# Down and row products issued as two matmuls of 256 columns in place of one of 512

## The chip, the cores and the metric

The kernel runs on one core of one Trainium2 chip. The metric is the device time of one execution in microseconds. Three runs of the kernel before gave 1739.73 to 1748.12 us, median 1745.62. Times in the profile are microseconds unless marked ns.

## The reference

One sequence of 256 tokens with 1024 features in float32 passes through two layers and then a second block. Cut to what matters here (the mixers between are recurrences, convolutions and attention over projections of the same kind):

```python
def swiglu(h, w_gate, w_up, w_down):
    return (jax.nn.silu(h @ w_gate) * (h @ w_up)) @ w_down        # 1024 -> 2816 -> 1024

for layer in range(2):                                            # first block
    x = x + 0.5 * swiglu(rmsnorm(x, norm_ffn1[layer]), ffn1_gate[layer], ffn1_up[layer], ffn1_down[layer])
    x = x + hybrid_mixer(rmsnorm(x, norm_mix[layer]), ...)
    x = x + 0.5 * swiglu(rmsnorm(x, norm_ffn2[layer]), ffn2_gate[layer], ffn2_up[layer], ffn2_down[layer])
h = rmsnorm(x, norm_final)                                        # second block, one layer
...                                                               # retention and dilated attention -> mixed
h = h + rmsnorm_2(mixed @ w_o[i], g_post_mix[i])
v2 = rmsnorm_2(h, g_pre_mlp[i])
f = jnp.square(jax.nn.relu(v2 @ w_up[i])) @ w_down[i]             # 1024 -> 4096 -> 1024
h = h + rmsnorm_2(f, g_post_mlp[i])
gate = jax.nn.sigmoid(rmsnorm_2(h, g_pre_ple[i]) @ w_ple_gate[i] + b_ple_gate[i])
e = p[i].astype(h.dtype) @ w_ple_in[i]
h = h + rmsnorm_2(gate * e, g_post_ple[i])
```

## The kernel before

**Products in three parts.** Every float32 operand of a large product is split into a rounded part and the rest (`xh`, `xl` for tokens, `wh`, `wl` for weights, type float32r), and a product is three matmuls: `xh wh + xh wl + xl wh`. `wchunk` (lines 86 to 95) brings weights in chunks of two k-tiles (2 x 128 rows, up to 512 columns, 512 KB): a DMA on SyncE's queue into one of four `raw` tiles, a cast on ScalarE to `wh` (line 93) and a subtraction on VectorE to `wl` (line 94), three pairs deep.

**Two ways to multiply.** `gemm_feat` (line 170) gives features on partitions: the stationary operand is a block of 128 weight columns, the moving one all 256 tokens, so each matmul has 256 columns; two outputs share a PSUM bank of 512 columns (lines 186 to 188). It is used for gate and up products of the FFNs, the MLP's up product and many projections. `gemm_tok` (line 121) gives tokens on partitions: the stationary operand is 128 tokens, the moving one up to 512 weight columns, so each matmul has 512 columns and fills a bank (lines 141 to 143 in `mm_tok`). Each matmul is issued with a weight load of its own, also where its stationary operand is the one before.

**Where the change touches.** Down products: `ffn` (line 314) runs four times; behind its feature products it computes two column halves of 512, each over 22 k-tiles and both token halves, with `gemm_tok` (line 348), and adds them to the residual. When the first column half is added, the next norm's transposes (line 279) of it can run, in the middle of the second half. Row products: `gemm_rows` (line 145) computes all 1024 columns into four banks, token half after token half in the last three chunks (`tail`), whose weights are kept in the room of hidden tiles (`hT`), so that the first token half is finished early. It is called for the output projection (`combine`, 8 k-tiles), the MLP's down product (`mlp`, 32 k-tiles) and the gate of the last part (`ple`, 8 k-tiles). All other users of `gemm_tok` (mixer and second block's projections, lines 571, 583, 1195, 1215, 1310 to 1358, 1420) keep their form.

**Order.** The program is written for a framework that tracks dependences, places instructions on the engines with a simulated timeline and the order of the program as priority, and adds the semaphores. TensorE runs its matmuls in the order placed.

Of the kernel before, what the change touches and what calls it, by code (L numbers as in the profile page):

```python
# [18 lines left out]
KC = 2  # L19
# [32 lines left out]
class Ctx:  # L52
# [65 lines left out]
        return self.m4.tile([P, 1040], F32, tag="m4", name=self.nm(name))  # L118


    def gemm_tok(self, xs, w, kt0, nkt, c0, n, outs=None, first=True, last=True, wk0=0):

        nc = self.nc
        xs = xs if isinstance(xs, list) else [xs]
        if outs is None:
            outs = [self.mm_tile() for _ in range(2)]
        for g in range(0, nkt, KC):
            m = min(KC, nkt - g)
            wh, wl = self.wchunk(w, (wk0 + g) * P, m, c0, n)
            for t in range(2):  # L130
                self.mm_tok(outs[t][:, :n], xs, kt0 + g, m, t, wh, wl, first and g == 0, last and g + m == nkt)
        return outs

    def mm_tok(self, o, xs, kt0, m, t, wh, wl, a, z):

        nc = self.nc
        tok = slice(t * P, (t + 1) * P)
        for k in range(m):
            xh, xl = xs[(kt0 + k) // 8]
            kt = (kt0 + k) % 8  # L140
            nc.tensor.matmul(o, xh[:, kt, tok], wh[:, k], start=a and k == 0, stop=False)  # L141
            nc.tensor.matmul(o, xh[:, kt, tok], wl[:, k], start=False, stop=False)  # L142
            nc.tensor.matmul(o, xl[:, kt, tok], wh[:, k], start=False, stop=z and k == m - 1)  # L143

    def gemm_rows(self, xs, w, nkt, tail, js):

        xs = xs if isinstance(xs, list) else [xs]
        outs = [[self.mm_tile() for _ in range(2)] for _ in range(2)]  # L150
        ng = nkt // KC
        for g in range(ng - tail):
            for ch in range(2):
                wh, wl = self.wchunk(w, g * KC * P, KC, ch * 512, 512)
                for t in range(2):
                    self.mm_tok(outs[ch][t], xs, g * KC, KC, t, wh, wl, g == 0, False)
        room = []
        for j in js:
            pair = [a.rearrange("p a b -> p (a b)").rearrange("p (i k c) -> p i k c", i=2, k=KC) for a in self.hT_tile(j)]
            room += [(pair[0][:, i], pair[1][:, i]) for i in range(2)]  # L160
        room += [None] * (2 * tail - len(room))
        ws = [[self.wchunk(w, g * KC * P, KC, ch * 512, 512, room.pop(0)) for g in range(ng - tail, ng)] for ch in range(2)]
        for t in range(2):
            for ch in range(2):
                for i, g in enumerate(range(ng - tail, ng)):
                    self.mm_tok(outs[ch][t], xs, g * KC, KC, t, *ws[ch][i], g == 0, g == ng - 1)
        return outs


# [136 lines left out]
def hidden_split(c, hT, hc, f0, nb):  # L306

    k0 = f0 // P
    h, l = hT[k0 // 8]
    k0 %= 8  # L310
    c.split(h[:, k0:k0 + nb], l[:, k0:k0 + nb], hc)


def ffn(c, st, wT, wg, wu, wd, F):


    nc = c.nc
    xs, r = st.norm_T(wT)
    between = []
    rbc = r_broadcast(c, r, between)  # L320
    rq = c.small.tile([P, 2], F32, tag="rr", name=c.nm("rr"))
    nc.vector.tensor_scalar(rq, r, 0.25, None, op0=ALU.mult)
    KF = F // P
    hT = [c.hT_tile(j) for j in range((KF + 7) // 8)]
    rb = bc(rbc.unsqueeze(1), [P, 2, S])
    for c0 in range(0, F, 512):
        n = min(512, F - c0)
        g = c.gemm_feat(xs, wg, 8, c0, n)
        gs = []

        def gate():
            for i in range(n // 256):
                gn, th = v2(c.w2("gn"), 2), v2(c.w2("th"), 2)
                nc.vector.tensor_tensor(gn, v2(g[i], 2), rb, op=ALU.mult)
                nc.scalar.activation(th, gn, AF.Tanh, scale=0.5)
                nc.vector.scalar_tensor_tensor(th, th, 1.0, gn, op0=ALU.add, op1=ALU.mult)
                gs.append(th)

        if c0 == 0:
            between.append(gate)  # L340
        else:
            gate()
        u = c.gemm_feat(xs, wu, 8, c0, n, between)
        for i in range(n // 256):
            nc.vector.tensor_tensor(gs[i], gs[i], v2(u[i], 2), op=ALU.mult)
            hidden_split(c, hT, gs[i], c0 + 256 * i, 2)
    for c0 in (0, 512):
        o = c.gemm_tok(hT, wd, 0, KF, c0, 512)
        for t in range(2):
            xx = st.x[:, t, c0:c0 + 512]  # L350
            nc.vector.scalar_tensor_tensor(xx, o[t], rq[:, t:t + 1], xx, op0=ALU.mult, op1=ALU.add)
# [38 lines left out]
def bc(ap, shape):  # L390
    return ap.broadcast_to(list(shape))
# [95 lines left out]
def r_broadcast(c, r, later=None):  # L487

    nc = c.nc
    ps = c.x_tile("rbc")  # L490
    h, l = (c.small.tile([P, 2, P], F32R, tag=n, name=c.nm(n), bufs=1) for n in ("dgh", "dgl"))
    for t in range(2):
        nc.scalar.activation(h[:, t], c.ident, AF.Copy, scale=r[:, t:t + 1])
        nc.vector.scalar_tensor_tensor(l[:, t], c.ident, r[:, t:t + 1], h[:, t].bitcast(F32), op0=ALU.mult, op1=ALU.subtract)
    o = c.small.tile([P, S], F32, tag="rbcs", name=c.nm("rbcs"))
    f = lambda a: a.rearrange("p a b -> p (a b)")
    nc.tensor.matmul(ps[:, :S], c.onesr, f(h), start=True, stop=False)

    def rest():
        nc.tensor.matmul(ps[:, :S], c.onesr, f(l), start=False, stop=True)  # L500
        nc.scalar.copy(o, ps[:, :S])

    rest() if later is None else later.append(rest)
    return o


def v2(ap, a):
    return ap.rearrange("p (a b) -> p a b", a=a)
# [985 lines left out]
def block_kernel(tc, a, layout):  # L1494
    with ExitStack() as stack:
        c = Ctx(tc, stack)
        nc = c.nc
        st = Stream(c, a["x"])
        cols = load_cols(c, a["col"], layout)
        for L in range(2):  # L1500
            wn = lambda n: cols[n][:, 8 * L:8 * L + 8]
            ffn(c, st, wn("norm_ffn1"), a["ffn1_gate"][L], a["ffn1_up"][L], a["ffn1_down"][L], D_FF)
            if L == 0:
                load_consts(c, a["tab"])
                prm = MixParams(c, cols, a, a)
                fq = c.const.tile([P, 9], F32, name="fq")
                o = TAB2_LAYOUT["invf"][0]
                nc.gpsimd.dma_start(fq, a["tab2"][:, o:o + 9])
                rope = Rope(c, a["pos_row"], a["pos_col"], fq[:, 0:1], fq[:, 1:9])
            Mixer(c, st, prm, a["w_in"][L], a["w_out"][L], L)  # L1510
            ffn(c, st, wn("norm_ffn2"), a["ffn2_gate"][L], a["ffn2_up"][L], a["ffn2_down"][L], D_FF)
        Block2(c, st, prm, a, rope)
# [41 lines left out]
```

## Time and profile before

| | |
|---|---|
| median of three runs | 1745.62 us |
| the profiled execution | 1734.22 us |
| its span, first to last instruction | 1732.4 us |
| TensorE matmuls / weight loads busy | 98% / 88% |
| VectorE, ScalarE busy | 68%, 53% |
| read from memory | 289 MB, 168 GB/s over the span |

A row of the page's groups has the line, engine and operation, what is written and read, the shape, the count, and then busy time and mean duration in ns. A matmul's recorded duration is longer than its distance to the next one, since matmuls are pipelined; the distance between starts gives the rate. PEld is the weight load, which can lie beside the matmul before it. Some matmul records can be missing.

### The profile page before, as it was taken

Reading aid. Unit: us, or ns where it says so; the run is one execution under the profiler, and the core shown is the slowest. Engines: PE = TensorE matmul, PEld = TensorE weight load, DVE = VectorE, ACT = ScalarE, POOL = GpSimd, SP = SyncE. Lnnn points to the kernel's source line nnn. Section 1 sums busy time; section 2 is a strip of 40 time slices with the busy share of each in tenths; the row PEclk is TensorE's granted clock in tenths of the full one; section 3 lists DMA queues with packets and bytes.
Section 4 is the critical chain, followed back from the end, with each engine's and each line's share of the span. In section 5 each row is a group of like instructions: output and inputs, shape, how many; then the busy total and the mean of one; then the engine's idle time right before and its main releaser. Section 6 shows DMA issues by size and latency. Waiting matters only on the chain.

```text
span 1732.4 us, 28619 instructions
## 1 busy us (share of the span) xinstructions
PE 1696.1 (98%) x11266; PEld 1529.2 (88%) x11266; DVE 1175.7 (68%) x2099; ACT 909.8 (53%) x1420; POOL 24.8 (1%) x62
## 2 busy tenths in 40 slices
PE   8999999999999999999989999999999999999996
PEld 7998899889988998899879998888888888799885
DVE  7666689776655765589866656656666665766467
ACT  5445576554444544568545445555454544555454
POOL 2000000100000000000000000000000000000000
PEclk9999999999999999999999999999999999999998
DMA  7657543345475656543435565554434456556661
GB/s 232 196 162 229 173 146 90 105 137 194 157 230 184 195 177 209 171 153 108 144 108 191 184 201 190 176 181 147 144 122 129 154 180 215 192 170 193 188 228 61
DMA packets 90503, 292.12 MB, mean 169 GB/s; under 512 B 9568, under 2 KB 22240, under 8 KB 90368
## 3 DMA queue, kind: packets, MB, share of 16 engines
q1 hardware_dynamic: 89648, 289.12, 51.6%
q8 instruction: 88, 1.44, 0.3%
q0 software_dynamic: 576, 1.07, 0.3%
q14 instruction: 47, 0.39, 0.1%
q10 hardware_dynamic: 144, 0.11, 0.0%
HBM read 289.21 MB, written 1.05 MB: 168 GB/s over the span
## 4 chain that ended last, share of the span: by engine, by line
PE 88%; DVE 5%; ACT 4%; issue 1%; DMA 1%; DVEq 0%; ACTq 0%
PE mm L141 14%; PE mm L142 13%; PE mm L143 13%; PE mm L187 13%; PE mm L188 13%; PE mm L186 13%; PE sv L730 1%; ACT wh L93 1%; DVE wl L94 1%; DMA raw<-in_weights 1%; PE pv L1268 1%; PE dsc L1236 1%; PE dsc L1235 1%; PE dpT L1254 0%; PE dS L677 0%
## 5 line engine op out<-in xcount | busy, mean ns | idle before, releaser
L94 DVE TENSOR_TENSOR wl<-raw,wh 128x1024 fp32r<-128x1024 f32 (+2 forms) x544 | 640.0, 1177 | 447.1 <-ACT wh L93 444.9
L93 ACT CAST wh<-raw 128x1024 fp32r<-128x1024 f32 (+2 forms) x544 | 550.4, 1013 | 608.1 <-PE mm L187 258.6
L186 PE MATMUL mm<-xTh,wh 128*128 128x256 f32 x2112 | 584.9, 279 | 4.0 <-ACT xTh L200 2.9
L187 PE MATMUL mm<-xTl,wh 128*128 128x256 f32 x2112 | 587.1, 279 | 1.3 <-DVE xTl L201 1.2
L188 PE MATMUL mm<-xTh,wl 128*128 128x256 f32 x2112 | 585.6, 279 | 0.1
L186 PEld LDWEIGHTS mm<-xTh,wh 128*128 128x128 f32 x2112 | 397.1, 189 | 8.4 <-ACT xTh L200 4.6
L187 PEld LDWEIGHTS mm<-xTl,wh 128*128 128x128 f32 x2112 | 398.2, 189 | 4.2 <-DVE xTl L201 3.1
L188 PEld LDWEIGHTS mm<-xTh,wl 128*128 128x128 f32 x2112 | 397.2, 189 | 2.1 <-issue 1.2
L142 PE MATMUL mm<-wl,hT 128*128 128x512 f32 x608 | 240.0, 395 | 0.0
L143 PE MATMUL mm<-wh,hT 128*128 128x512 f32 x608 | 237.1, 392 | 0.0
L141 PE MATMUL mm<-wh,hT 128*128 128x512 f32 x608 | 218.4, 395 | 2.8 <-ACT hT L200 2.7
L142 PE MATMUL mm<-wl,xTh 128*128 128x512 f32 (+1 forms) x440 | 168.9, 385 | 0.0
L143 PE MATMUL mm<-wh,xTl 128*128 128x512 f32 (+1 forms) x440 | 165.7, 382 | 0.1
L141 PE MATMUL mm<-wh,xTh 128*128 128x512 f32 (+1 forms) x440 | 160.0, 383 | 1.5 <-ACT xTh L200 1.5
L141 PEld LDWEIGHTS mm<-wh,hT 128*128 128x128 f32 x608 | 114.5, 189 | 28.3 <-ACT hT L200 3.5
L143 PEld LDWEIGHTS mm<-wh,hT 128*128 128x128 f32 x608 | 114.7, 189 | 25.5 <-DVE hT L201 0.9
L142 PEld LDWEIGHTS mm<-wl,hT 128*128 128x128 f32 x608 | 114.7, 189 | 24.0
L141 PEld LDWEIGHTS mm<-wh,xTh 128*128 128x128 f32 x440 | 82.0, 188 | 18.3 <-ACT xTh L200 2.4
L142 PEld LDWEIGHTS mm<-wl,xTh 128*128 128x128 f32 x440 | 82.8, 188 | 16.4 <-issue 1.9
L143 PEld LDWEIGHTS mm<-wh,xTl 128*128 128x128 f32 x440 | 82.4, 188 | 16.5 <-issue 2.0
L200 ACT ACTIVATE xTh<-xtr,colp 128x256 fp32r<-128x256 f32 (+1 forms) x72 | 28.9, 450 | 14.0 <-DVE xTl L201 12.4
L201 DVE SCALAR_TENSOR_TENSOR xTl<-xtr,colp,xTh 128x256 fp32r<-128x256 f32 (+1 forms) x72 | 30.5, 448 | 3.7 <-ACT xTh L200 3.4
(456 smaller groups left out, 1590.0 us busy)
## 6 DMA issues: line engine op xcount, KB each, us to landing
raw<-in_weights SPq DMA_DIRECT2D x514, 512.0 KB, 3.4
raw<-in_weights SPq DMA_DIRECT2D x32, 256.0 KB, 3.2
raw<-in_weights SPq DMA_DIRECT2D x16, 260.0 KB, 3.2
x_res<-in_x SPq DMA_DIRECT2D x4, 256.0 KB, 5.9
rowp<-in_b_gate SPq DMA_DIRECT2D x2, 512.0 KB, 4.0
out<-pg SPq DMA_DIRECT2D x4, 256.0 KB, 2.1
tab<-in_tab SPq DMA_DIRECT2D x1, 900.5 KB, 5.4
ctab<-in_tab POOLq DMA_DIRECT2D x1, 643.0 KB, 6.4
```

The lines of the kernel that those rows point to most:

```text
L93: nc.scalar.copy(h, raw)
L94: nc.vector.tensor_tensor(l, raw, h.bitcast(F32), op=ALU.subtract)
L141: nc.tensor.matmul(o, xh[:, kt, tok], wh[:, k], start=a and k == 0, stop=False)
L142: nc.tensor.matmul(o, xh[:, kt, tok], wl[:, k], start=False, stop=False)
L143: nc.tensor.matmul(o, xl[:, kt, tok], wh[:, k], start=False, stop=z and k == m - 1)
L186: nc.tensor.matmul(o, wh[:, k, cs], xh[:, kt], start=a, stop=False)
L187: nc.tensor.matmul(o, wh[:, k, cs], xl[:, kt], start=False, stop=False)
L188: nc.tensor.matmul(o, wl[:, k, cs], xh[:, kt], start=False, stop=z)
L200: nc.scalar.activation(h, src, AF.Copy, scale=scale)
L201: nc.vector.scalar_tensor_tensor(l, src, scale, h.bitcast(F32), op0=ALU.mult, op1=ALU.subtract)
L730: nc.tensor.matmul(o[:, h], lhsT[:, h], rhs[:, h], start=True, stop=True)
L1235: nc.tensor.matmul(ps[:, 0:P], q[:, 0:P], k[:, 0:P], start=True, stop=True)
```

## The change

`mm_tok` gets a number of pieces, `cut`; with `cut=2` each matmul of 512 columns becomes two of 256 columns, with the same stationary operand, into the two halves of the same bank. The start mark stands on the first piece of a bank's first product alone, the stop mark on the last piece of its last. `gemm_tok` passes `cut` on (default 1); the down products and both loops of `gemm_rows` ask for 2.

```diff
-    def gemm_tok(self, xs, w, kt0, nkt, c0, n, outs=None, first=True, last=True, wk0=0):
+    def gemm_tok(self, xs, w, kt0, nkt, c0, n, outs=None, first=True, last=True, wk0=0, cut=1):
...
-                self.mm_tok(outs[t][:, :n], xs, kt0 + g, m, t, wh, wl, first and g == 0, last and g + m == nkt)
+                self.mm_tok(outs[t][:, :n], xs, kt0 + g, m, t, wh, wl, first and g == 0, last and g + m == nkt, cut)
...
-    def mm_tok(self, o, xs, kt0, m, t, wh, wl, a, z):
+    def mm_tok(self, o, xs, kt0, m, t, wh, wl, a, z, cut=1):
...
+        n = o.shape[1] // cut
         for k in range(m):
             xh, xl = xs[(kt0 + k) // 8]
             kt = (kt0 + k) % 8
-            nc.tensor.matmul(o, xh[:, kt, tok], wh[:, k], start=a and k == 0, stop=False)
-            nc.tensor.matmul(o, xh[:, kt, tok], wl[:, k], start=False, stop=False)
-            nc.tensor.matmul(o, xl[:, kt, tok], wh[:, k], start=False, stop=z and k == m - 1)
+            for i, (xx, ww) in enumerate(((xh, wh), (xh, wl), (xl, wh))):
+                for j in range(cut):
+                    cs = slice(j * n, (j + 1) * n)
+                    nc.tensor.matmul(o[:, cs], xx[:, kt, tok], ww[:, k, cs], start=a and k + i + j == 0,
+                                     stop=z and k == m - 1 and i == 2 and j == cut - 1)
...
-                    self.mm_tok(outs[ch][t], xs, g * KC, KC, t, wh, wl, g == 0, False)
+                    self.mm_tok(outs[ch][t], xs, g * KC, KC, t, wh, wl, g == 0, False, 2)
...
-                    self.mm_tok(outs[ch][t], xs, g * KC, KC, t, *ws[ch][i], g == 0, g == ng - 1)
+                    self.mm_tok(outs[ch][t], xs, g * KC, KC, t, *ws[ch][i], g == 0, g == ng - 1, 2)
...
-        o = c.gemm_tok(hT, wd, 0, KF, c0, 512)
+        o = c.gemm_tok(hT, wd, 0, KF, c0, 512, cut=2)
```

## Rows read from the trace of the kernel before

**Rows 1.** The page: span, and TensorE's busy time, share and instructions.

```profile
span 1732.4 us, 28619 instructions
...
PE 1696.1 (98%) x11266; PEld 1529.2 (88%) x11266; DVE 1175.7 (68%) x2099; ACT 909.8 (53%) x1420; POOL 24.8 (1%) x62
```

**Rows 2.** The page: busy tenths and granted clock in 40 equal slices.

```profile
PE   8999999999999999999989999999999999999996
...
PEclk9999999999999999999999999999999999999998
```

**Rows 3.** TensorE's waits: total us, times, longest us.

```profile
PE xtr L279 <- POOL ident L78: 4.9, 1, 4.9
...
PE mm L141 <- ACT hT L200: 2.7, 2, 1.4
```

**Rows 4.** Busy us (x instructions) of each engine, clock, DMA share, GB/s, by stretch.

```profile
134.70:196.00 61.30, 61.30 (x274) 50.32 (x273) 36.22 (x57) 29.61 (x40) 0.00 (x0) 1.00 0.61 188
...
1603.00:1691.20 88.20, 88.20 (x386) 72.11 (x386) 49.07 (x55) 41.79 (x46) 0.00 (x0) 1.00 0.64 208
```

**Rows 5.** Chain of waits in the first down product: start us, us, what.

```profile
140.38 0.46 PE mm L141 x2
...
170.59 0.46 PE mm L141 x2
```

**Rows 6.** Timeline of TensorE, three row products: start us, us, engine, line, operation.

```profile
1603.06 0.39 PE L141 MATMUL mm<-wh,hT 128*128 128x512 f32 x1
...
1691.03 0.40 PE L143 MATMUL mm<-hT,hT 128*128 128x512 f32 x1
...
1498.41 0.40 PE L141 MATMUL mm<-hT,hT 128*128 128x512 f32 x1
...
1505.88 0.40 PE L143 MATMUL mm<-hT,hT 128*128 128x512 f32 x1
...
1704.97 0.39 PE L142 MATMUL mm<-wl,xTh 128*128 128x512 f32 x1
...
1708.89 0.39 PE L142 MATMUL mm<-hT,xTh 128*128 128x512 f32 x1
```

**Rows 7.** Timeline of TensorE in the first FFN: feature products, then the down product.

```profile
103.78 0.28 PE L186 MATMUL mm<-xTh,wh 128*128 128x256 f32 x1
...
109.90 0.28 PE L186 MATMUL mm<-xTh,wh 128*128 128x256 f32 x1
...
134.61 0.28 PE L188 MATMUL mm<-xTh,wl 128*128 128x256 f32 x1
134.72 0.62 PE L141 MATMUL mm<-wh,hT 128*128 128x512 f32 x2
```

**Rows 8.** Timeline of TensorE: feature products behind other matmuls, two runs.

```profile
1308.61 0.28 PE L186 MATMUL mm<-xTh,wh 128*128 128x256 f32 x1
...
1312.97 0.28 PE L187 MATMUL mm<-xTl,wh 128*128 128x256 f32 x1
...
545.04 0.28 PE L186 MATMUL mm<-xTh,wh 128*128 128x256 f32 x1
...
547.75 0.28 PE L188 MATMUL mm<-xTh,wl 128*128 128x256 f32 x1
```

**Rows 9.** Timeline of TensorE: token products of 260 columns, seven starts.

```profile
196.54 0.28 PE L141 MATMUL mm<-wh,xTh 128*128 128x260 f32 x1
...
197.26 0.28 PE L142 MATMUL mm<-wl,xTh 128*128 128x260 f32 x1
```

**Rows 10.** The page's groups: matmuls and loads of one line of the feature products.

```profile
L187 PE MATMUL mm<-xTl,wh 128*128 128x256 f32 x2112 | 587.1, 279 | 1.3 <-DVE xTl L201 1.2
...
L187 PEld LDWEIGHTS mm<-xTl,wh 128*128 128x128 f32 x2112 | 398.2, 189 | 4.2 <-DVE xTl L201 3.1
```

**Rows 11.** Timeline of TensorE: transposes in the middle of a down product.

```profile
176.84 0.38 PE L279 MATMUL xtr<-ident,x_res 128*128 128x128 f32 x2
176.97 0.48 PE L142 MATMUL mm<-wl,hT 128*128 128x512 f32 x1
```

## The prediction, made before the change was run

> **What bounds the kernel now.** I read the page's busy line first, then the clock line, TensorE's waits, the busy time by stretch, and then single starts in the timeline, since the change is about the pace of single matmuls. TensorE is busy 1696.1 of 1732.4 us, so it is idle for 36.3 us in all [rows 1], at the full clock in nearly every slice [rows 2]; its longest single wait is 4.9 us, at the very start, and what it waits for at a down product is 2.7 us in the whole run [rows 3]. In the stretches that the change touches TensorE has no idle time at all: 61.30 of 61.30 us in a down product and 88.20 of 88.20 us in the MLP's row product, at granted clock 1.00 (the 2.4 GHz level), while VectorE is busy 36.22 and 49.07 us and DMA has a share of 0.61 and 0.64 [rows 4]. So the weights arrive with room, and a nanosecond more or less per matmul there goes straight into the time. A busy TensorE says nothing about its rate, though; the rate is the distance from one start to the next, and that is what has to be read.
>
> **How many.** From the code, matmuls of 512 columns that are cut: four FFNs x 2 column halves x 22 k-tiles x 2 token halves x 3 products = 1056; the row products with 8, 32 and 8 k-tiles x 2 x 2 x 3 = 96 + 384 + 96. Together 1632, each becoming two of 256 columns with a weight load of its own: 1632 more matmuls and 1632 more loads. No DMA, no activation, no vector instruction and no wait is added; the two halves write the same bank, one after the other, so no one further back is let go earlier or later by construction.
>
> **What a 512-column matmul costs now.** Down product: eleven weight chunks of 12 matmuls lie between the pieces at 140.38 and 170.59 us, so 30.21 us / 132 = 228.9 ns [rows 5]. MLP row product: 384 starts from 1603.06 to 1691.03 us, 87.97 / 383 = 229.7 ns. Output row product's tail: 33 starts from 1498.41 to 1505.88, 7.47 / 32 = 233.4 ns. Gate row product: 18 starts from 1704.97 to 1708.89, 3.92 / 17 = 230.6 ns [rows 6].
>
> **What a 256-column one costs.** The trace has it in the feature products, with a new load for each: 55 starts from 103.78 to 109.90 us, 6.12 / 54 = 113.3 ns, so a pair is 226.7 ns [rows 7]. That is less than one matmul of 512 columns, by 2.2 to 6.7 ns. But there is a second pace: 38 starts from 1308.61 to 1312.97 are 4.36 / 37 = 117.8 ns apart, and 24 from 545.04 to 547.75 are 2.71 / 23 = 117.8 ns apart [rows 8]; a pair is then 235.7 ns, dearer than the 512. In the trace a run of feature products keeps the pace with which it sets out: the long runs that nothing interrupts hold 113.3, short ones that begin behind other matmuls show either. This is the uncertain part, as the halves stand in both situations. The moving operand differs too (weights instead of tokens). The nearest row with weights moving is the 260-column product, at 0.72 / 6 = 120.0 ns [rows 9]; taken for 256 columns it is the upper end, and 113.3 is the lower.
>
> **The second load.** The two halves have the same stationary operand, and it is loaded twice. The feature products already do this: lines 186 and 187 load the same weight columns one after the other, with 2112 matmuls and 2112 loads on line 187, so equal loads are not merged, and they still go at 113.3 ns [rows 7, 10]. So I cost the loads at nothing beside the 256 columns that cover them; without that cover the 4.5 ns between the two paces is the price.
>
> **The sum.** Matmuls that follow a feature product without a break: 158 in each FFN up to its first transposes (about 171 us in the first), 632 in all, and the 384 of the MLP; the down product of the first FFN begins 0.11 us behind the last feature matmul [rows 7]. At the fast pace they give 632 x 2.2 + 384 x 3.0 = 1.4 + 1.2 = 2.5 us. The other 616 come behind transposes, which put TensorE out of step (the 512 behind a pair of them begins 0.13 us after it and lasts 0.48 instead of 0.39 us [rows 11]): 424 in the FFNs, 96 and 96 in two row products. At the fast pace they give 424 x 2.2 + 96 x 6.7 + 96 x 3.9 = 1.9 us, at the slow pace they cost 424 x 6.8 + 96 x 2.3 + 96 x 5.1 = 3.6 us. With nothing to choose between them I take the middle, 0.8 us lost. That makes 1.7 us gained, rounded to 2: the profiled execution would go from 1734.2 us (span 1732.4 and 1.8 around it) to 1732. That execution lies 11.4 us under the median of the runs, 1745.6; the same 2 us from the median gives 1743.6, and I say 1743. Both paces together bound this at 4.4 us gained and 1.1 lost. What is late next is TensorE still: per chunk the down stretch leaves VectorE 25 us in 61 unused [rows 4].
>
> **Instruction order.** The builder places instructions by a simulated timeline, in which two halves need not cost what one whole does. The order of transposes, casts and loads in and behind these stages may therefore move, and the mixers after them too. I put it at nothing, since TensorE has no idle time there to lose or win [rows 4]. From both sides it is bounded by the 36.3 us of idle time [rows 1]: a better order can win a part of it, a worse one can add as much; 10 us either way is my estimate, about a quarter of it.
>
> **A rule that speaks against the change.** Two paces of the trace, 113.3 at 256 and 228.9 at 512, leave no fixed cost per matmul: doubling the first is 2.2 below the second [rows 5, 7]. The Trainium skill ("TensorE: Matmul & The Clock Gate", section "Back-to-back issue gap") has it the other way: a warm matmul in isolation costs its columns at 2.4 GHz and about 2.5 ns on top, whatever its length. By that the change would pay 1632 x 2.5 = 4.1 us (an estimate from that page). The pairs in this trace do not agree with it, but they were measured with another moving operand.
>
> **The rivals.**
> *The slow pace everywhere (the other side).* In all five places the halves lock at 117.8 ns, because the load of one half and the stream of the other get out of step where the moving operand is weights. Cost: 632 x 6.8 + 384 x 6.0 + 3.6 = 4.3 + 2.3 + 3.6 = 10.2 us, so 1756, slower. It decides once the halves' mean passes 117.4 ns, where 1632 pairs have cost 8.7 us. For it: the 120.0 of the 260-column product [rows 9]. Against it: every long run of 256 columns in the trace is fast [rows 7].
> *A fixed cost per half.* If each start costs something of its own, halves lie between the two paces, at 115.6: 231.1 a pair, (231.1 - 229.5) x 1632 = about 3 us lost, 1748. Against it is the comparison of 113.3 with 228.9.
> *A better or worse order.* The planner's new timeline moves casts or transposes in the mixers: 10 us either way, 1735 or 1755. For it: much of the 36.3 us of idle time lies outside the cut products. Against it: no dependence changes.
> *The change doesn't do what it says.* If the second load were left out, a pair could drop below 226.7 and gain more than 4.4 us. The equal counts of loads and matmuls [rows 10] speak against it; I fold it into the better order.
>
> **How the numbers follow.** Forecast (mixed pace, 1739 to 1747): 0.58. Fixed cost: 0.11. Slow pace: 0.12. Better order: 0.14; worse order: 0.05. Half a per cent, about what can be told from no change, is 8.7 us: under 1736.9 or over 1754.3. Faster: the better order and a little of the forecast's spread, 0.16. Slower: the slow pace and the worse order, less what stays under the bound, 0.15. Within: 0.69. The runs shown spread by 8.4 us themselves, so the range goes from 1732 to 1756.
>
> **What would show it.** The matmuls of the down products with 128x256 operands, twice as many, starting 113.3 ns apart; behind the transposes of the second half of a down product 113.3 or 117.8, one of the two for the whole run. The first down stretch (61.3 us now) should be 60.7 to 61.5 us, and TensorE's loads as busy as its matmuls in it. A mean over 117 ns, a down stretch over 62 us, idle time on TensorE within it, or a time outside 1736.9 to 1754.3 would make the forecast wrong.

## The result, and the profile after

The changed kernel takes **1761.48 us** (median of 6 runs, 1757.86 to 1765.44) against 1740.62 us of the kernel before (6 runs, 1735.13 to 1748.12). The ratio is 1.0124, 95% interval 1.0102 to 1.0145. It is slower by about 21 us, where I forecast 1743 us and no change; the range ended at 1756.

The profiled execution is the one that took 1761.61 us. Its page, the span, TensorE's busy line and the clock line, beside [rows 1, 2]:

```profile
span 1759.7 us, 31881 instructions
PE 1713.8 (97%) x12898; PEld 1613.0 (92%) x12898; DVE 1177.7 (67%) x2099; ACT 912.5 (52%) x1422; POOL 25.0 (1%) x62
PEclk9999999799999999999999999999999999999999
```

The span is 27.3 us longer than in [rows 1]. The profiled execution of before (1734.22 us) lies below its median and this one does not, so the two traces stand further apart than the medians. TensorE is busy 17.7 us longer and idle 9.6 us longer (45.9 against 36.3). The eighth slice of the clock line, which was a 9 [rows 2], is a 7.

**In the first down product the changed products went at the faster of the two forecast paces.** The timeline of TensorE at both ends of the first down product, whose last products stand directly before the transposes of the next norm:

```profile
134.81 0.28 PE L192 MATMUL mm<-xTh,wl 128*128 128x256 f32 x1
134.92 0.62 PE L146 MATMUL mm<-wh,hT 128*128 128x256 f32 x4
135.38 0.39 PE L146 MATMUL mm<-wl,hT 128*128 128x256 f32 x2
...
194.54 0.40 PE L146 MATMUL mm<-wh,hT 128*128 128x256 f32 x2
194.77 1.91 PE L283 MATMUL xtr<-ident,x_res 128*128 128x128 f32 x16
197.09 0.39 PE L146 MATMUL mm<-wh,xTh 128*128 128x260 f32 x1 [0.42 <-ACT xTh L204]
...
199.16 0.39 PE L146 MATMUL mm<-wh,xTh 128*128 128x260 f32 x1 [0.80 <-ACT xTh L204]
```

From 134.92 to 194.77 lie 528 halves: 59.85 us / 528 = 113.4 ns, so a pair costs 226.7, against 228.9 for one whole product [rows 5]. But the fence shows something else. All 16 transposes of the next norm stand in one block **behind** the down product. Before, the first eight stood in the middle of its second column half (two of them in [rows 11]), and ScalarE and VectorE split them while the products went on. Now TensorE waits for the split (0.42 and 0.80 us).

The stretches that got longer are others. Busy time by stretch (length, busy us of TensorE, its loads, VectorE, ScalarE and GpSimd with their counts, granted clock, DMA share, GB/s), from one residual sum to the next: first mixer, feature and first down products of the second layer's first FFN, second mixer. Before:

```profile
197.00:360.90 163.90, 159.68 (x1190) 148.78 (x1188) 141.47 (x322) 106.39 (x208) 7.15 (x17) 0.99 0.38 120
546.10:697.30 151.20, 151.20 (x1196) 145.54 (x1195) 99.45 (x124) 74.11 (x93) 0.00 (x0) 1.00 0.59 192
728.40:893.50 165.10, 159.30 (x1189) 148.04 (x1188) 141.64 (x325) 105.82 (x209) 3.07 (x9) 0.99 0.39 128
```

After:

```profile
195.70:371.60 175.90, 170.01 (x1197) 158.20 (x1195) 144.09 (x326) 107.51 (x211) 6.86 (x17) 0.93 0.36 112
555.30:712.30 157.00, 155.43 (x1339) 154.63 (x1338) 101.14 (x128) 75.39 (x97) 0.00 (x0) 0.99 0.57 185
743.40:918.00 174.60, 164.93 (x1197) 153.04 (x1195) 144.60 (x329) 109.77 (x214) 3.54 (x9) 0.96 0.38 120
```

The two mixers, in which no product was cut, are 12.0 and 9.5 us longer, the FFN stretch 5.8: together 27.3, the whole difference (the rest adds up to nothing). Length times what the clock lacks of 1.00, and length less TensorE's busy time, divide it (the clock is given to two digits, so a product with it is good to about 0.9 us):

- First mixer: at the clock 175.9 x 0.07 = 12.3 us against 163.9 x 0.01 = 1.6, so 10.7 more; idle 5.9 against 4.2, 1.7 more. Sum 12.4 of 12.0.
- Second mixer: 7.0 against 1.7, 5.3 more; idle 9.7 against 5.8, 3.9 more. Sum 9.2 of 9.5.
- FFN stretch: idle 1.6 against none; clock 1.6 against none; its first down half went at the slow pace, 132 x 6.8 = 0.9; the rest is work that used to stand in front of it, as eight of the transposes did.

The largest piece is the clock, in a stretch of the first mixer. The kernel before, and then the changed one, at the same place:

```profile
306.00:336.00 30.00, 30.00 (x197) 27.16 (x196) 25.33 (x51) 19.54 (x48) 4.24 (x10) 0.94 0.34 109
```

```profile
305.00:335.00 30.00, 30.00 (x155) 27.68 (x155) 17.61 (x39) 12.92 (x34) 5.09 (x12) 0.66 0.27 89
```

TensorE is busy 30.00 of 30.00 us in both, yet 155 matmuls lie in the stretch instead of 197, and those that start in it have 21592 columns instead of 35892: by its granted clock of 0.66 TensorE ran at its lower level (1.2 of 2.4 GHz) for two thirds of the time. The busy time of the loads does not show it either (27.68 against 27.16). What TensorE did before the first fall, in the changed kernel's timeline:

```profile
303.50 0.28 PE L146 MATMUL mm<-wh,xTl 128*128 128x260 f32 x1
303.62 0.40 PE L146 MATMUL mm<-wh,xTh 128*128 128x260 f32 x2
303.86 0.97 PE L734 MATMUL sv<-hS,LTm 128*128 128x32 f32 x8
304.76 1.16 PE L955 MATMUL hS<-hA,hB 64*128 64x128 f32 x8
305.85 0.39 PE L146 MATMUL mm<-wl,xTh 128*128 128x260 f32 x1
306.08 0.98 PE L734 MATMUL sv<-hS,LTm 128*128 128x32 f32 x8
...
308.37 0.42 PE L146 MATMUL mm<-wl,xTh 128*128 128x260 f32 x1
308.59 0.42 PE L146 MATMUL mm<-wh,xTl 128*128 128x260 f32 x1
```

Between 303.86 and 306.89 us stand 24 short links of the mixer's recurrence, products of 32 and 128 columns, and one wide product. The granted clock is 1.00 up to 307 us, 0.52 from 307 to 310, mostly 1.00 again up to 314 and 0.50 from there to 326; the wide products of 260 columns start 0.12 us apart before (303.50 and 303.62) and 0.22 us apart at the lower level (308.37 and 308.59). TensorE is busy without a break in all of it. The idle part is in TensorE's waits (total us, times, longest us), where the 2.7 us of the second line of [rows 3] stands unchanged beside these:

```profile
PE mm L146 <- ACT xTh L204: 4.8, 6, 1.4
PE mm L190 <- ACT xTh L204: 4.4, 8, 0.9
PE sv L734 <- ACT hS L761: 3.9, 3, 1.5
PE yT L842 <- DVE yth L985: 2.9, 1, 2.9
```

The first two are products that wait for the split of the norm's transposes (1.5 and 2.9 us in the kernel before), the last two are waits inside the mixers (0.8 us and none before).

### The profile page after: what moved, and what is told of

The parts are those of the page before. It is cut to its first block, busy times and chain, and to the rows that moved or that the text cites. A ratio compares the mean times of both kernels' runs of the same rounds, so it can differ in the third digit from the quotient of the medians.

```text
span 1759.7 us, 31881 instructions
## 1 busy us (share of the span) xinstructions
PE 1713.8 (97%) x12898; PEld 1613.0 (92%) x12898; DVE 1177.7 (67%) x2099; ACT 912.5 (52%) x1422; POOL 25.0 (1%) x62
## 4 chain that ended last, share of the span: by engine, by line
PE 92%; ACT 4%; DVE 2%; DMA 1%; issue 1%; SPq 0%; DVEq 0%; ACTq 0%
PE mm L146 42%; PE mm L191 13%; PE mm L192 13%; PE mm L190 13%; PE sv L734 2%; DMA raw<-in_weights 1%; ACT wh L93 1%; PE dS L681 1%; PE pv L1272 1%; PE dsc L1240 1%; DVE wl L94 1%; ACT junk L258 1%; PE hS L931 1%; ACT xTh L204 1%; PE dsc L1239 1%
## 5 line engine op out<-in xcount | busy, mean ns | idle before, releaser
L146 PE MATMUL mm<-wh,hT 128*128 128x256 f32 (+1 forms) x2144 | 385.2, 295 | 2.7 <-ACT hT L204 2.7
L146 PEld LDWEIGHTS mm<-wh,hT 128*128 128x128 f32 x2144 | 303.0, 189 | 16.8 <-ACT hT L204 3.5
L146 PE MATMUL mm<-wl,hT 128*128 128x256 f32 (+1 forms) x1072 | 239.9, 294 | 0.0
L146 PEld LDWEIGHTS mm<-wl,hT 128*128 128x128 f32 x1072 | 168.7, 189 | 6.0
L146 PE MATMUL mm<-wl,xTh 128*128 128x512 f32 (+2 forms) x448 | 169.5, 382 | 0.0
L146 PE MATMUL mm<-wh,xTl 128*128 128x512 f32 (+2 forms) x448 | 166.7, 380 | 1.0 <-DVE xTl L205 0.9
L146 PE MATMUL mm<-wh,xTh 128*128 128x512 f32 (+2 forms) x448 | 161.9, 382 | 4.8 <-ACT xTh L204 4.8
L146 PE MATMUL mm<-hT,hT 128*128 128x256 f32 x288 | 34.3, 279 | 0.3 <-ACT hT L201 0.3
L146 PEld LDWEIGHTS mm<-hT,hT 128*128 128x128 f32 x288 | 33.7, 188 | 0.5 <-ACT hT L201 0.5
L349 DVE TENSOR_TENSOR th<-th,mm 128x512 f32<-128x512 f32 x44 | 28.8, 684 | 3.2 <-PE mm L192 2.7
```

The source lines that it names most:

```text
L146: nc.tensor.matmul(o[:, cs], xx[:, kt, tok], ww[:, k, cs], start=a and k + i + j == 0, stop=z and k == m - 1 and i == 2 and j == cut - 1)
```

## The experiments

My theory, **A**: the planner set the same work in another order, and that order costs the time, in the mixers above all; the halves cost nothing. The rival, **B**: halved products cost something themselves that the trace puts elsewhere. All ratios are against the kernel before on the same chip. A kernel's runs spread by 7 to 19 us, so the mean over all its runs of span x (1 - clock), here "at the clock", and of span x clock, "the rest", is listed beside the medians. The difference to before, of the rounded means, is in brackets, in each column with a 95% interval of 2 to 4 us to either side; the changed kernel, whose own partner runs have no clock listed, is set against the 26 runs of before that went with the second table half.

```
kernel              runs  median   ratio, 95% interval       at the clock   the rest
changed                6  1761.48  1.0124 [1.0102, 1.0145]   23.5 (+10.1)   1736.2 (+10.9)
halves_norm_early     12  1742.57  1.0011 [0.9991, 1.0031]   13.8 (+0.3)    1727.3 (+1.8)
wholes_norm_late       6  1771.85  1.0168 [1.0139, 1.0198]   29.8 (+16.3)   1740.4 (+14.9)
rows_only             12  1740.53  0.9999 [0.9980, 1.0019]   14.2 (+0.7)    1726.0 (+0.5)
c0_only               12  1740.02  0.9983 [0.9959, 1.0008]   13.8 (+0.3)    1723.2 (-2.3)

c512_only              4  1759.52  1.0113 [1.0077, 1.0148]   22.8 (+9.4)    1734.2 (+8.9)
early_mixers           9  1750.04  1.0060 [1.0036, 1.0084]   14.4 (+1.0)    1735.3 (+10.0)
early_ffn              8  1752.14  1.0079 [1.0050, 1.0108]   22.1 (+8.7)    1730.1 (+4.8)
halves_calm           12  1739.90  1.0006 [0.9979, 1.0033]   11.7 (-1.7)    1726.2 (+0.9)

halves_first5         12  1743.19  0.9997 [0.9973, 1.0021]   12.5 (+0.5)    1729.6 (-0.5)
halves_last6           8  1756.34  1.0076 [1.0050, 1.0103]   22.2 (+10.2)   1733.7 (+3.6)
```

The kernel before ran beside the three groups at medians of 1739.74, 1741.20 and 1744.31 us.

**All halves, the old order (halves_norm_early).** The edit gives the transposes of a norm's first half behind a down product a place 250 earlier in the planner's order of priority:

```diff
+    def early(self, half, steps):
+        by = 0 if half else self.lead
+        self.lead, self.tc.cur_priority = 0, self.tc.cur_priority - by
+        yield from steps
+        self.tc.cur_priority += by
-                for kp in range(2):
+                for kp in c.early(half, range(2)):
# ffn, behind the residual sum of a down product:
+            c.lead = 250
```

> The changed kernel, and the transposes of the next norm's first half get a priority 250 instructions earlier behind each down product, so that the planner puts them into its second column half again, as in the kernel before. Theory A (the order that the planner makes costs the time, the halves themselves do not): 1731 to 1742 us, 0.995 to 1.001 of before (1740.6), the first mixer back at about 164 us between the residual sums. Theory B (the halves cost the time, by their second loads, the slow pace of 117.8 ns and the clock): 1753 to 1762 us, as the changed kernel.

1742.57 us, half a microsecond over A's range and no difference to before that can be told. The transposes are back in the middle (timeline):

```profile
176.39 0.27 PE L285 MATMUL xtr<-ident,x_res 128*128 128x128 f32 x1
...
178.24 0.27 PE L285 MATMUL xtr<-ident,x_res 128*128 128x128 f32 x1
...
197.11 0.38 PE L285 MATMUL xtr<-ident,x_res 128*128 128x128 f32 x2
```

So 1632 halved products cost nothing that can be told from the spread (the interval goes from 1.6 us gained to 5.4 lost); B, which asked for 1753 to 1762 us, falls, and what costs depends on the order. One thing that I expected did not come: the first mixer of the profiled execution is not back at 164 us (the two mixers, from sum to sum):

```profile
196.10:364.90 168.80, 164.44 (x1190) 153.25 (x1189) 141.46 (x322) 106.15 (x207) 7.06 (x17) 0.96 0.36 117
734.90:901.10 166.20, 160.29 (x1190) 149.31 (x1188) 141.74 (x325) 105.69 (x208) 3.07 (x9) 0.98 0.39 128
```

Its clock is 0.96, so the old order too can lose at the clock in a single execution; over the runs the loss is that of before (+0.3 us).

**No halves, the late norm (wholes_norm_late).** All cuts are undone. An addition of zero times a product of the second column half to four elements of each sum of the first makes the transposes wait for the end of the down product:

```diff
# ffn, and the same 2 to 1 in the row products:
-        o = c.gemm_tok(hT, wd, 0, KF, c0, 512, cut=2)
+        o = c.gemm_tok(hT, wd, 0, KF, c0, 512, cut=1)
...
+    for t in range(2):
+        nc.vector.scalar_tensor_tensor(st.x[:, t, 0:512:128], o[t][:, 0:4], 0.0, st.x[:, t, 0:512:128],
+                                       op0=ALU.mult, op1=ALU.add)
```

> No halves at all: the kernel before, with eight values per FFN of the first column half of the residual written once more (plus zero times the second product), so that the next norm's first transposes must wait for the end of the down product, as they do in the changed kernel. Theory A: 1757 to 1768 us, 1.010 to 1.016 of before, each mixer 9 to 12 us longer, granted clock falling in them. Theory B: 1739 to 1743 us, as before.

1771.85 us: without a single half the kernel is slower than the changed one. It is worse than the 1768 I allowed: the added operation itself makes TensorE wait (0.41 us behind this down product, timeline), and the two mixers are 15.7 and 13.8 us longer than before where 9 to 12 were expected (stretches from sum to sum). Why they lose more than in the changed kernel is open:

```profile
198.17 1.53 PE L283 MATMUL xtr<-ident,x_res 128*128 128x128 f32 x12 [0.41 <-DVE x_res L355]
```

```profile
198.10:377.70 179.60, 171.69 (x1200) 159.74 (x1200) 144.32 (x327) 109.27 (x217) 6.85 (x17) 0.92 0.34 109
755.40:934.30 178.90, 168.47 (x1200) 156.79 (x1200) 144.59 (x330) 111.39 (x220) 3.54 (x9) 0.94 0.36 118
```

**One part alone: the row products (rows_only), and the first column half (c0_only).** In both the transposes stay where they were.

```diff
# rows_only: the down products whole, the three row products in halves
+        o = c.gemm_tok(hT, wd, 0, KF, c0, 512, cut=1)
# c0_only: the row products whole, and
+        o = c.gemm_tok(hT, wd, 0, KF, c0, 512, cut=1 if c0 else 2)
```

> Halves in the three row products alone (576 of the 1632 matmuls); the down products whole. Theory A: the FFNs and mixers as before, 1737 to 1743 us. Theory B: 576/1632 of the 20.9 us lost, 7 us, so about 1748 us.

> Halves in the first column half of the down products alone (528 of the 1632 matmuls), where no other work waits for a place; second half and row products whole. Theory A: 528 x 2.2 ns = 1.2 us gained, 1738 to 1741 us. Theory B: 528/1632 of 20.9 us lost, 7 us, so about 1747 us.

Both are as before (0.9999 and 0.9983). In c0_only the halves go at 113.3 ns in all four FFNs (263 distances each), and each down product, from its first matmul to the first one behind it, is 0.3 us shorter (61.0 against 61.3), as 132 x 2.2 ns makes it. That is 1.2 us in all four, which no ratio here can show.

**The second column half alone (c512_only).**

```diff
# the row products whole, and in ffn
+        o = c.gemm_tok(hT, wd, 0, KF, c0, 512, cut=2 if c0 else 1)
```

> Halves only in the second column half of the down products, during which the next norm's transposes may be placed; first column half and the three row products whole. As built, the transposes stand behind the whole down product, as in the changed kernel. Theory A (the order is what costs): nearly the whole loss, 1756 to 1765 us, ratio 1.009 to 1.014, the two mixers 17 to 25 us longer together, TensorE at half clock for 25 us or more outside the tail. Theory B (the halves cost by their number, all five places alike): 528 of 1632 halved products, a third of 21 us, 1745 to 1749 us.

1759.52 us: a third of the halves carries the whole loss, as A says and B does not. These are the halves among which the planner may place the next norm. The clock line has a low slice in each mixer:

```profile
PEclk9999999899999999999899999999999999999999
```

**Which norm (early_mixers, early_ffn).** All halves, with the earlier place only for the norm in front of a mixer, or only for the one behind a second FFN:

```diff
# ffn takes lead and sets it behind the residual sum; early_mixers:
+            ffn(c, st, wn("norm_ffn1"), ..., D_FF, 250)
# early_ffn:
+            ffn(c, st, wn("norm_ffn2"), ..., D_FF, 250)
```

> The changed kernel with all its halves; only the transposes of the norm behind a first FFN (the one that feeds a mixer) get an earlier priority, so they stand in the middle of that down product as before. Behind the second FFNs they stay at the end. Theory A1 (the loss is made in the mixers): mixers within 6 us of before, the 21 us there come back and the 6 us of the next layer's feature products stay: 1742 to 1749 us, ratio 1.002 to 1.005. Theory A2 (the late norm costs the same wherever it is, three sites alike, about 9 us each): about 1749 to 1752 us. Theory B (halves): 1757 to 1762 us.

> The counterpart: the earlier priority only behind a second FFN (the norm that feeds the next layer's feature products, and the last norm), the transposes in front of a mixer stay behind the whole down product. Theory A1 (the loss is made in the mixers): 1753 to 1760 us, mixers 17 to 25 us longer together than before, feature products of the second layer within 1.5 us of before. Theory A2 (three sites alike): about 1749 to 1754 us. Theory B (halves): 1757 to 1762 us, with the 6 us in the feature products still there.

Both medians, 1750.04 and 1752.14, fit A2 (every site costs, each about alike) and just miss A1 (the mixers make nearly the whole loss). The table says more than the medians: with the mixers' order back, the loss at the clock is gone (+1.0 us) and only "the rest" stays (+10.0); with the mixers' late order it is the other way (+8.7 and +4.8). Taken over halves_norm_early (+0.3, +1.8), and each with the intervals said above, the mixers' order costs 8.4 at the clock and 3.0 in the rest, the other norms 0.7 and 8.2; with the +0.3 and +1.8 that makes 9.4 and 13.0 against 10.1 and 10.9 measured for the changed kernel. So there are two losses of similar size: one in the mixers, mostly clock, and one that comes with the late norms behind the second FFNs, mostly not. The mixers of early_mixers (stretches as above), then those of early_ffn:

```profile
196.40:359.20 162.80, 158.43 (x1190) 147.37 (x1188) 141.25 (x322) 106.04 (x207) 7.20 (x17) 1.00 0.37 120
542.90:698.40 155.50, 153.78 (x1339) 152.92 (x1338) 100.97 (x128) 75.24 (x97) 0.00 (x0) 1.00 0.57 187
730.40:897.10 166.70, 160.88 (x1190) 149.46 (x1188) 141.75 (x325) 105.94 (x208) 3.07 (x9) 0.98 0.39 127
```

```profile
203.40:370.80 167.40, 161.49 (x1198) 150.15 (x1195) 143.63 (x326) 107.09 (x211) 7.10 (x17) 0.99 0.37 117
556.50:708.40 151.90, 151.90 (x1332) 151.90 (x1332) 99.41 (x124) 74.14 (x93) 0.00 (x0) 1.00 0.58 191
739.40:921.70 182.30, 173.73 (x1198) 161.32 (x1195) 144.45 (x330) 109.91 (x214) 3.55 (x9) 0.91 0.36 116
```

The middle row follows its own site: 155.50 us with 1.72 idle where the norm is late, 151.90 with none where it is early. The mixers with the late order are 3.5 and 17.2 us longer than before in this execution and 12.0 and 9.5 in the one of the changed kernel: the clock falls now in the one, now in the other.

**Is it the late start of a mixer, or the order inside it? (halves_first5, halves_last6)** Halves only in the second column half of the down products, there only in the first 5 or the last 6 of 11 weight chunks:

```diff
# gemm_tok, called with cut=2 if c0 else 1; halves_first5:
+                self.mm_tok(..., last and g + m == nkt, cut if g < 10 else 1)
# halves_last6:
+                self.mm_tok(..., last and g + m == nkt, cut if g >= 10 else 1)
```

> Halves in the second column half of the down products only, there only in the first 5 of 11 weight chunks (240 products over the four FFNs). As built, the next norm's first transposes stand some 48 matmuls later than before, still inside the down product, and the order of VectorE in the mixers is that of before. Theory A (the order costs): 1739 to 1744 us, mixers within 3 us of before each, granted clock as before. Theory B (the halves cost by number: 240 of the 528 that cost 18 us): 1748 us.

> The counterpart: only the last 6 of 11 chunks in halves (288 products). As built, 7 of the 8 transposes of the norm's first half stand in the middle of the down product where they stood before, one stands behind it; the mixers have the same changed order of VectorE and ScalarE as the changed kernel. Theory A-order (the changed order inside the mixers lowers the granted clock there, wherever the transposes stand): 1748 to 1758 us, mean granted clock under 0.990, mixers 14 us or more longer together. Theory A-late (the mixers lose because their input arrives late): 1740 to 1746 us, mixers within 6 us together, clock 0.992. Theory B (halves by number: 288 of the 528 that cost 18 us): 1750 us, but with the loss inside the down products.

240 halved products cost nothing (0.9997), 288 cost 0.76%. In the second kernel seven of the eight transposes of the norm's first half stand in the middle of the down product (four more at 169.83), and only one is behind it, with the next half's right behind that (timeline):

```profile
175.78 0.38 PE L283 MATMUL xtr<-ident,x_res 128*128 128x128 f32 x2
...
178.77 0.27 PE L283 MATMUL xtr<-ident,x_res 128*128 128x128 f32 x1
...
195.37 0.27 PE L283 MATMUL xtr<-ident,x_res 128*128 128x128 f32 x1
...
196.92 1.04 PE L283 MATMUL xtr<-ident,x_res 128*128 128x128 f32 x8
```

Yet the order of VectorE in the mixers is close to that of the changed kernel, and the loss at the clock is the same: +10.2 us over 8 runs. The traces show this for every kernel. I laid VectorE's instructions of each mixer, in order of their starts, beside those of the kernel before and counted the ones outside the longest common order (321 to 325 instructions in the first mixer, 325 to 329 in the second):

```
kernel              moved in the mixers   at the clock
changed                  53,  79             +10.1
wholes_norm_late         51,  70             +16.3
c512_only                52,  70              +9.4
early_ffn                53,  74              +8.7
halves_last6             51,  72             +10.2

halves_norm_early         0,   4              +0.3
rows_only                 0,   0              +0.7
c0_only                   0,   4              +0.3
early_mixers              0,   0              +1.0
halves_calm               0,   4              -1.7
halves_first5             0,   0              +0.5
```

But for 16 instructions at most the mixers have one of two orders, and the loss at the clock goes with the second of them, whether the products are halved or not and whether seven of the eight transposes stand in the middle or none. That is theory A-order, whose time and clock halves_last6 also has (1756.34 us, 0.987). The profiled execution of halves_last6 is the fastest of its eight (clock 0.992); its second mixer shows the loss, and its first does not, so the 14 us that I expected of the two together were not there (9.0):

```profile
196.30:360.50 164.20, 158.29 (x1191) 147.43 (x1189) 142.68 (x324) 106.73 (x209) 7.10 (x17) 1.00 0.38 120
...
735.10:908.90 173.80, 165.02 (x1191) 153.72 (x1189) 143.94 (x328) 109.45 (x212) 3.55 (x9) 0.95 0.38 122
```

**Halves only where nothing stands between them (halves_calm):** c0_only with the MLP's row product (384 products) in halves too.

```diff
# gemm_rows, over c0_only:
-                    self.mm_tok(outs[ch][t], xs, g * KC, KC, t, wh, wl, g == 0, False, 1)
+                    self.mm_tok(outs[ch][t], xs, g * KC, KC, t, wh, wl, g == 0, False, 1 + (nkt == 32))
# and the same in the last chunks
```

> Halves only where no other TensorE work stands between them: the first column half of each down product and the MLP's row product (528 + 384 products); the second column half, the output and the gate row products whole. As built, the order of VectorE and ScalarE differs from before in 44 lines. Theory A (pace gives 2.2 to 3.0 ns per product where the order is kept): 528 x 2.2 + 384 x 3.0 = 2.3 us gained in those stretches, 1737 to 1740 us against 1740 before, ratio 0.9975 to 1.000. Rival (each half costs something of its own): 1741 to 1744 us.

1739.90 us, 1.0006 [0.9979, 1.0033]. Its trace has the forecast paces (113.3 ns in the four down products, 113.8 in the MLP's), but a gain of 2.3 us (0.13%) lies inside that interval, and so does none; the halves are worth nothing that the times can show. No kernel here is shown to beat the one before.

## Why the prediction was wrong

- **The pace of the halves: right in size, not in where it falls.** In the changed kernel's trace the first, second and fourth FFN go at 113.3 ns throughout, the third at 117.8 (522 distances from 680.96 us on); the MLP at 113.8, the output product at 118.9 in its first chunk and 117.8 in its tail. The gate product, at 120 in most of its distances, is slower than both forecast paces. I counted products that follow a feature product without a break as fast; the third FFN's do follow one, and after two distances of 210 and 227 ns (from 680.40 us) they were slow to the end. Behind transposes I took the middle, "with nothing to choose between them"; the traces choose: where the transposes stand in the middle of a wholly halved down product (four times in halves_norm_early, twice each in early_mixers and early_ffn), the halves behind them go at 118.2 to 118.4 ns in all eight.
- **The sum of the halves: a small gain was forecast, a small loss is likelier.** halves_norm_early has all the halves in the order that I had in mind. Its interval, from 1.6 us gained to 5.4 lost, just leaves out the 1.7 gained. In its profiled execution the four down products take 0.1, 1.9, 0.4 and 0.4 us more than before and the gate product 0.6 more; the MLP's product takes 0.8 less and the stretch of the output product 0.6 less, with four transposes fewer in it. That is about 2 us lost, where I had put the bound at 1.1. (The first down stretch by my own terms could go up to 61.7 us, not 61.5; it took 61.4, the second 63.2.) With one profile of each kernel, a loss of 2 us is shown for that execution alone. Of the 21 us it explains little.
- **The second load: right.** Every half has a load of its own (12898 matmuls and 12898 loads), and at 113.3 ns the loads cost nothing beside the columns. The Trainium skill ("TensorE: Matmul & The Clock Gate", section "Back-to-back issue gap") gives a warm matmul in isolation 2.5 ns on top of its columns; the pairs at the fast pace do not agree, 226.7 against 228.9.
- **Instruction order: this is the step that failed.** "I put it at nothing, since TensorE has no idle time there to lose or win", and the bound was "10 us either way", a quarter of the idle time. Two things are wrong with it. The first: "there" was the down product, but what moved out of it, the transposes of the next norm, came together with another order inside the mixer behind it, in which nothing was cut. That was among the rivals ("The planner's new timeline moves casts or transposes in the mixers") with 0.05 and against it "no dependence changes". No dependence is needed: in halves_last6 one transpose of the first eight stands behind the down product, and 51 and 72 of VectorE's instructions in the two mixers are in another order. The second: idle time does not bound a loss of order. The changed kernel's order costs 21 us in the medians, and about half of it, 10.1 us by the runs' clocks, is lost with TensorE at 1.2 GHz, where it mostly shows as **busy**. In [rows 3] and [rows 4] nothing can be read of that; the mixers' clock by stretch was there to be read (0.94 at 306 to 336 us) and I read only the stretches of the change. I also misread the 2.7 us of [rows 3]: its two waits lie one in each mixer, at the mixer's own output product, and none at a down product.
- **The rivals.** "Slow pace everywhere" gave the right side and 1756 us for a wrong reason: the slow pace came in one FFN, the output product and the gate product, and not in the rest. "Fixed cost per half" falls with the 113.3. The worse order (1755) is what happened, at twice its price, and it had a chance of 0.05.
- **What would show it.** I named idle time within the down stretch; there was none. The sign was one line further, in what stands behind it.

**Open.** Why the planner moves the transposes to the end when the last products are in halves is not shown; its timeline is not in a trace. Nor is it shown what in the new order of the mixers lowers the clock: that the recurrence has fewer wide products beside it is a guess, and an experiment that fills the stretch with more of them was not made. Of "the rest" behind the second FFNs (8.2 us by the runs) the trace of early_mixers shows 4.3 in the middle row above; what it shows beyond that is 1.9 us of idle time where the norm behind the last FFN now is late, and 1361 products of the MLP in one run, from 1524.5 to 1684.7 us, at 117.8 ns, which at 113.5 would have taken about 6 us less. How often such a run falls into the slow pace a single profile per kernel does not give, so how much of the 8.2 us is order and how much pace is open.

## What to carry to other kernels

Where a planner places instructions by a simulated timeline, a change that leaves every dependence alone can still move work that it never touches: compare the instruction order of the two builds beyond the changed stretch first, and price what moved at the place where it is needed, not where it stood. Idle time is no bound for a bad order, since TensorE at half its clock shows as busy (30.00 of 30.00 us at 0.66); multiply every stretch by its granted clock before saying what is at stake. To separate a change from the order that came with it, pin the old order and keep the change, and undo the change and keep the new order.

## What the runs showed of the hardware that I had not expected

- **Busy at half speed.** 30.00 of 30.00 us busy at a granted clock of 0.66, 21592 columns against 35892, with the loads' busy time at 27.68 against 27.16. In place of the matmuls' busy share, the Trainium skill ("Perfetto Trace Analysis", section "Identifying the Most-Contended Engine") asks for the share of the peak's operations and the busy share of the loads; in this stretch the second of them is as blind as the matmuls' own.
- **The same products go at either pace.** In the profiled execution of early_ffn the whole first FFN, its 1056 feature products and the down product behind them, went at the slow pace, where the same feature products of the kernel before went at the fast one, over 1000 distances in either; the first down product's 528 halves, up to the transposes, are (202.48 - 140.29) / 528 = 117.8 ns apart (timeline):

```profile
140.29 0.64 PE L146 MATMUL mm<-wh,hT 128*128 128x256 f32 x4
...
202.24 0.40 PE L146 MATMUL mm<-wh,hT 128*128 128x256 f32 x2
202.48 0.71 PE L285 MATMUL xtr<-ident,x_res 128*128 128x128 f32 x5
```

  That FFN came to its first sums 6.4 us later than before, of which the two paces explain about 1020 x 4.5 ns + 132 x 6.8 ns = 5.5 us. These are two kernels with one profile each; whether the pace also changes between executions of one kernel no run here shows.
- **The kernel before loses to the clock too:** 13.4 us in the mean over 26 runs, at clocks between 0.988 and 0.996. Its spread of 17.7 us goes with that in part (correlation of span and loss 0.70), and what moves the clock from run to run is open.
